# Slots of 2048 bytes and four wide ones, contraction rows padded to 128, and a hand order for the first instructions

## The chip, the cores and the metric

The kernel runs on one core of one Trainium2 chip. The metric is the device time of one execution in microseconds (us). The engines are named as the profile names them: PE (matrix engine) with PEld (its weight loads), DVE (vector), ACT (scalar), POOL, and SP, which here only issues transfers. A matmul multiplies a stationary operand (loaded into PE first) by a moving operand that streams through column by column.

## What is computed

Three blocks over 256 tokens of width 1024, all in float32: two transformer-like layers, then a third with a state-space mixer.

```python
for i in range(2):
    x = x + 0.5 * swiglu(rms_norm(x, g1[i]), w_in1[i], w_out1[i])        # hidden width 2816
    hn = rms_norm(x, gm[i])
    # layer 0: mLSTM, 4 heads of 128 (values 256); layer 1: windowed attention, 16 query and 2 key heads of 64
    y = concat(token_heads(hn @ w_a_or_b), memory_heads(xq, mem_k, mem_v))
    x = x + y @ w_o[i]
    x = x + 0.5 * swiglu(rms_norm(x, g2[i]), w_in2[i], w_out2[i])
h = x + hybrid_mixer(rmsnorm(x))     # state-space scan of 32 heads, short convolutions, gates
h = h + swiglu_2(rmsnorm(h))
return rmsnorm(h)
```

In the windowed attention each of two 128-token blocks scores `s = q k^T` per head, masks it, takes a softmax with a sink, and multiplies by the values. In the state-space scan every head needs `exp(min(acum[l] - acum[s], 0))`, for which one row of cumulative decays per head is spread over all partitions.

## The kernel before, in words

**Weights and products.** Every weight matrix is cut into chunks of up to [128, 1024] float32. `load` (L313) issues a chunk's transfer on SP into one of five `raw` tiles; `prepare` (L321) makes two parts of it, `whi` (ACT copy, rounded to fp32r, L329) and `wlo` (DVE subtraction, L330 through the helper at L122). Activations are split in the same way. A product is three fp32r matmuls: hi·hi, hi·lo, lo·hi. In `gemm` (L396) the activation is stationary and 512 weight columns move (L423 to L425); in `gemm_ch` (L434) the weights are stationary and 256 tokens move (L445 to L447); in `gemm_hidden` (L564) they are stationary and the hi and lo activations move side by side (L574, 512 columns) or the hi ones alone (L575, 256).

**Where operands lie.** SBUF is dealt out in the order of the pools: constants, `wpool` (raw, whi, wlo, 4096 bytes each per partition), `xtp` (two `xt` tiles of 8192 bytes, the transposed normalised activations), `sp` (31 slots under one tag "s"), small tiles. A tag's slots all have the size of its widest tile. `slot()` asks for 512 floats, 2048 bytes, but `v_evac` (L844) asks the same tag for 514 floats, 2056 bytes, so the slots stand more than 2056 bytes apart, while whi, wlo and xt stand at multiples of 2048 bytes from each other. A stationary piece is 128 floats, so pieces within a tile are 512 bytes apart. Products whose activation is a transposed, normalised input take it from `xt`; those after a hidden layer, an attention or a gate take it from slots (`operand_block`, L463).

**Order.** Nothing loops at run time. The Python order is a priority; the Tile scheduler orders the instructions of each engine, adds the waits, and hands a slot to a tile when one is free. Small work (attention, scan) is put between the gemms' matmuls by hand-set paces: `tick` (L365) after every second weight entry, `defer(n, ...)` for n ticks later, `later` and `pipeline` for generators.

**The first instructions** (L751 to L776): `load_x(0)` and two rows of gains on SP, two chunks by `prepare(2)` (which also issues six chunk loads), `load_x(1)` behind them on SP, 8 + 12 warm-up matmuls on PE (L762), the spread of the gains (L766), and per 128 tokens `norm_residual`: squares on ACT (L523), a power on POOL (L513), two scalings on DVE (L131), four transposes and a split per half (L454 to L461). `ffn_in` then takes its first eight chunks as one group: all eight for the first 128 tokens, then all for the others.

**Small contractions.** A matmul's contraction rows are its operands' partitions. Three kinds use fewer than 128: the windowed scores (L1061, 64 rows, plain float32; heads of one parity per unit, since even heads lie in partitions 0 to 63 of the transposed queries and odd ones in 64 to 127), the spread of the mLSTM stabiliser (L857, 4 rows), and the spread of the decays (L1278, 64 rows, fp32r). L1278 runs in 16 units of two matmuls, L1061 in 16 units of two or four, L857 once in each of 4.

Of the kernel before, what the change touches and what calls it, by code (L numbers as in the profile page):

```python
# [27 lines left out]
WBUFS = 9  # L28
N_SLOTS = 31
PACE_A = 0.5  # L30
# [55 lines left out]
def hybrid_kernel(ctx: ExitStack, tc: tile.TileContext, *aps, names=None):  # L86
# [7 lines left out]
    xtp = ctx.enter_context(tc.tile_pool(name="xtp", bufs=2))  # L94
    sp = ctx.enter_context(tc.tile_pool(name="sp", bufs=N_SLOTS))
    tp = ctx.enter_context(tc.tile_pool(name="tp", bufs=1))
    mm = ctx.enter_context(tc.tile_pool(name="mm", bufs=4, space=PSUM))
# [4 lines left out]
    def nm(s):  # L102
        uid[0] += 1
        return f"{s}_{uid[0]}"

    def slot(dtype=F32):
        return sp.tile([P, 512], dtype, tag="s", name=nm("s"))

    def tiny():
# [34 lines left out]
    identr = const.tile([P, P], F32R, name="identr")  # L144
    act.copy(out=identr, in_=ident)
    ones = const.tile([P, P], F32, name="ones")
# [174 lines left out]
    def prepare(upto):  # L321
        while prepared[0] < min(upto, len(plan)):
            c = plan[prepared[0]]
            load(prepared[0] + RAW)
            prepared[0] += 1
            c.hi = wpool.tile([P, 1024], F32R, tag="whi", bufs=WBUFS, name=nm("whi"))
            c.lo = wpool.tile([P, 1024], F32R, tag="wlo", bufs=WBUFS, name=nm("wlo"))
            n = max(off + w for _, _, off, w in c.entries)
            act.copy(out=c.hi[:, 0:n], in_=c.raw[:, 0:n])  # L329
            tt(c.lo[:, 0:n], c.raw[:, 0:n], c.hi[:, 0:n].bitcast(F32), ALU.subtract)  # L330

# [130 lines left out]

    def operand_block(op, tok, k0, src, nk, delay=2):  # L463
        def go():
            hi, lo = slot(F32R), slot(F32R)
            split_t(src, nk, [x[:, 0:nk * P].rearrange("p (a b) -> p a b", a=nk) for x in (hi, lo)])
            for i in range(nk):
                op.parts[tok, k0 + i] = (hi[:, i * P:(i + 1) * P], lo[:, i * P:(i + 1) * P])
        defer(delay, go)
# [111 lines left out]

    def ffn_in(blocks, xop):

# [3 lines left out]
        def evac(t, key, ps):  # L587
            if key == "g":
                keep[t] = slot()
                act.activation(out=keep[t], in_=ps, func=AF.Silu)  # L590
            else:
                tt(keep[t], keep[t], ps, ALU.mult)
                operand_block(h, t, 0, keep[t], 4, D_FFN)
        gemm(blocks[0], xop, evac, [blocks[0][0:FIRST], blocks[0][FIRST:]] if FIRST < 8 else [blocks[0]])

# [158 lines left out]
    for j in range(2):  # L754
        nc.sync.dma_start(out=g_row[j * 32:j * 32 + 1, :], in_=A["ffn1_norm_g"][0:1, j * 512:(j + 1) * 512])
    prepare(2)
    load_x(1)
    warm = bank()

    def warm_up(n):  # L760
        for _ in range(n):
            pe.matmul(out=warm[:, 0:P], lhsT=ones, rhs=ones, start=True, stop=True)  # L762
    warm_up(WARM[0])
    for j in range(2):
        gains.append(bank())
        pe.matmul(out=gains[j], lhsT=ones[j * 32:j * 32 + 1, :], rhs=g_row[j * 32:j * 32 + 1, :], start=True, stop=True)  # L766

    warm_up(WARM[1])

    def fill(t):  # L770
        norm_residual(t, gains, xop)
    for t in range(2):
        fill(t)
    defer(30, lambda: later(load_parameters()))
    pace[0] = 0.25
    h = ffn_in(S["f1in0"], xop)  # L776
    xop, fill = norm_after(A["mix_norm_g"][0])
# [19 lines left out]
    gg, efloor, fcum = little(), little(), little()  # L797
    m_t = slot()

    def gate_chain():  # L800
# [43 lines left out]
    def v_evac(t, key, ps):  # L844
        s = sp.tile([P, 514], F32, tag="s", name=nm("v"))
        act.copy(out=s[:, 1:513], in_=ps)
        pool_e.memset(s[:, 0:1], 1.0)
        pool_e.memset(s[:, 513:514], 1.0)
        v_t[t, int(key[1])] = s

    def score_head(hh):
        while len(k_t) <= hh // 2:
# [3 lines left out]
        bc = bank()  # L856
        pe.matmul(out=bc[:, 0:SEQ], lhsT=ident[0:4, hh:hh + 1].to_broadcast([4, P]), rhs=m_t[0:4, 0:SEQ],  # L857
                  start=True, stop=True)
# [147 lines left out]
    pace[0] = PACE_B  # L1006
    bkt, bv = slot(), slot()
    kv_ready = set()
    qts = {}

    def kv_evac(t, key, ps):
# [8 lines left out]
        def go():  # L1020
            tk = transposes(kd, 2)
            dve.tensor_copy(out=bkt.rearrange("p (g t) -> p g t", g=2)[:, :, t * P:(t + 1) * P],
                            in_=tk[:, 0:SEQ].rearrange("p (g t) -> p g t", g=2))
            kv_ready.add(t)
        defer(D_KV, go)

    def bq_evac(g):
        def evac(t, key, ps):
            qn = qk_norm(ps, t, 8, b_gq)

            def go():
                tq = transposes(qn, 4)
                q = slot()
                act.copy(out=q, in_=tq)
                qts[t, g] = q
            defer(D_ROPE, go)
        return evac

    def swa_units(t, g):
# [4 lines left out]
        mask = mask_w[:, 1, :] if t == 0 else mask_w.rearrange("p a b -> p (a b)")  # L1044
        sets = [[h0 + par + 2 * i for i in range(per)] for h0 in range(0, 8, 2 * per) for par in range(2)]
        sk = sinks[:, 8 * g:8 * g + 8]
        hold = {}

        def unit(n, hs):
            while (t, g) not in qts or len(kv_ready) <= t:  # L1050
                yield
            qt = qts[t, g]
            if not hold:
# [3 lines left out]
            o = slot()  # L1057
            cols = slice(hs[0], hs[-1] + 1, 2)
            for i, hh in enumerate(hs):
                half = slice(64 * (hh % 2), 64 * (hh % 2) + 64)  # L1060
                pe.matmul(out=s[:, i * w:(i + 1) * w], lhsT=qt[half, (hh // 2) * P:(hh // 2 + 1) * P],  # L1061
                          rhs=bkt[half, g * SEQ:g * SEQ + w], start=True, stop=True)
            for i, hh in enumerate(hs):
# [50 lines left out]
    def z_evac(half):  # L1114
        def evac(t, key, ps):
            s = slot()
            act.activation(out=s, in_=ps, func=AF.Silu)
            sz[t, 2 * half + int(key[1])] = s
        return evac
    gemm(S["z0"], xop, z_evac(0), [S["z0"][0:FIRST], S["z0"][FIRST:]] if FIRST < 8 else [S["z0"]])  # L1120

    dt_, acum, toend, eac, dtr = little(), little(), little(), little(), little()
    acs = const.tile([P, 2, 2, 32], F32R, name="acs")
    act_t = const.tile([64, SEQ], F32R, name="act_t")
    pick = const.tile([64, 32], F32R, name="pick")

# [17 lines left out]
    def step_chain():  # L1144
# [29 lines left out]
        for c in range(2):  # L1174
            pe.matmul(out=at_[0:64, c * P:(c + 1) * P], lhsT=acs[:, c, :, :].rearrange("p b c -> p (b c)"), rhs=identr,
                      start=True, stop=True)
        act.copy(out=act_t, in_=at_[0:64, 0:SEQ])
        tt(pick, ident[0:64, 0:32], ident[0:64, 32:64], ALU.add)
        steps_done.append(True)
# [88 lines left out]
    def ssd_unit(g, hp):  # L1268
# [7 lines left out]
        for i in range(2):  # L1276
            hd = 8 * g + 2 * hp + i
            pe.matmul(out=sb[:, i * SEQ:(i + 1) * SEQ], lhsT=pick[:, hd:hd + 1].to_broadcast([64, P]), rhs=act_t,  # L1278
                      start=True, stop=True)
# [168 lines left out]
```

## Time and profile before

| | us |
|---|---|
| median of 3 runs (lowest, highest) | 1605.06 (1604.77, 1608.36) |
| the profiled execution | 1604.94 |
| its span, first to last instruction | 1603.2 |
| PE busy | 1583.9 (99%) |
| DVE busy | 1037.7 (65%) |
| ACT busy | 886.1 (55%) |
| POOL busy | 39.7 (2%) |

Matmuls overlap and their ends are modelled, so PE's busy share says that it always had work, not how fast it went; for that one reads the distance from one matmul's start to the next one's. The granted clock was 0.999 of full speed over the span.

### The profile page before, as it was taken

What the parts mean: (1) busy time and instruction counts of PE and PEld (TensorE: products, weight loads), DVE (VectorE), ACT (ScalarE), POOL (GpSimd) and SP (SyncE); (2) the same over time, 40 slices, a digit from 0 to 9 for tenths busy, and PEclk for the clock granted to TensorE, in tenths of its full rate; (3) what the DMA queues carried; (4) which work ended last, traced back from release to release, by engine and by line L of the source; (5) the groups of instructions that cost most, each with busy time, mean ns of one, the idle gap of its engine ahead of it and who ended that gap; (6) DMA issues with size and microseconds to landing.
All of it is one profiled execution on the core that took longest, in us unless ns stands there. A gap on an engine that the chain in (4) does not pass through costs nothing.

```text
span 1603.2 us, 22953 instructions
## 1 busy us (share of the span) xinstructions
PE 1583.9 (99%) x8664; PEld 1355.3 (85%) x8664; DVE 1037.7 (65%) x1632; ACT 886.1 (55%) x1430; POOL 39.7 (2%) x72
## 2 busy tenths in 40 slices
PE   8999999999999999999999999999999999999998
PEld 7888897788888888887788888889899988888886
DVE  6676475657765567747765676468788864577662
ACT  6665365546655455635565655357855653456542
POOL 1000000100000000001100000000000000000000
PEclk9999999999999999999999999999999999999999
DMA  8656374446556546564323666465455566565560
GB/s 281 196 179 229 117 261 143 151 132 210 174 194 223 179 163 202 193 215 165 119 79 115 200 200 223 143 217 180 146 157 154 151 195 185 157 211 170 197 223 28
DMA packets 126467, 282.89 MB, mean 176 GB/s; under 512 B 11774, under 2 KB 23186, under 8 KB 126356
## 3 DMA queue, kind: packets, MB, share of 16 engines
q1 hardware_dynamic: 126356, 281.43, 54.6%
q8 instruction: 68, 1.11, 0.3%
q14 instruction: 43, 0.35, 0.1%
HBM read 280.34 MB, written 1.05 MB: 176 GB/s over the span
## 4 chain that ended last, share of the span: by engine, by line
PE 93%; DVE 2%; issue 1%; DMA 1%; ACT 1%; POOL 1%; SPq 0%; POOLq 0%; DVEq 0%; ACTq 0%
PE ps L574 20%; PE ps L423 15%; PE ps L425 15%; PE ps L424 15%; PE ps L575 11%; PE ps L445 3%; PE ps L446 3%; PE ps L447 3%; PE ps L458 2%; PE ps L1061 1%; PE ps L1303 1%; PE ps L676 1%; POOL t L517 1%; DVE wlo L122 1%; PE ps L1083 1%
## 5 line engine op out<-in xcount | busy, mean ns | idle before, releaser
L122 DVE TENSOR_TENSOR wlo<-raw,whi 128x1024 fp32r<-128x1024 f32 (+1 forms) x521 | 626.2, 1212 | 228.9 <-ACT whi L329 222.3
L329 ACT CAST whi<-raw 128x1024 fp32r<-128x1024 f32 (+1 forms) x521 | 537.5, 1042 | 321.8 <-PE ps L425 226.6
L574 PE MATMUL ps<-xt,whi 128*128 128x512 f32 x1440 | 500.6, 392 | 0.0
L575 PE MATMUL ps<-xt,wlo 128*128 128x256 f32 x1440 | 403.2, 280 | 0.0
L574 PEld LDWEIGHTS ps<-xt,whi 128*128 128x128 f32 x1440 | 269.4, 187 | 59.1
L423 PE MATMUL ps<-whi,s 128*128 128x512 f32 x696 | 277.4, 400 | 0.3 <-ACT s L1380 0.3
L424 PE MATMUL ps<-wlo,s 128*128 128x512 f32 x696 | 274.4, 394 | 0.0
L425 PE MATMUL ps<-whi,s 128*128 128x512 f32 x696 | 274.1, 394 | 0.0
L575 PEld LDWEIGHTS ps<-xt,wlo 128*128 128x128 f32 x1440 | 272.2, 189 | 0.2
L122 DVE TENSOR_TENSOR s<-ps,s 128x256 f32<-128x256 f32 (+1 forms) x218 | 101.3, 468 | 120.3 <-ACT s L600 100.8
L423 PE MATMUL ps<-whi,xt 128*128 128x512 f32 (+2 forms) x448 | 174.2, 389 | 3.2 <-ACT xt L460 1.8
L425 PE MATMUL ps<-whi,xt 128*128 128x512 f32 (+2 forms) x448 | 170.1, 381 | 1.2 <-DVE xt L122 1.2
L424 PE MATMUL ps<-wlo,xt 128*128 128x512 f32 (+2 forms) x448 | 169.8, 379 | 0.0
L423 PEld LDWEIGHTS ps<-whi,s 128*128 128x128 f32 x696 | 130.8, 188 | 31.4 <-DVE s L122 0.8
L425 PEld LDWEIGHTS ps<-whi,s 128*128 128x128 f32 x696 | 130.7, 188 | 30.7
L424 PEld LDWEIGHTS ps<-wlo,s 128*128 128x128 f32 x696 | 130.9, 188 | 28.7
L445 PE MATMUL ps<-xt,whi 128*128 128x256 f32 x448 | 129.1, 288 | 0.0
L122 DVE TENSOR_TENSOR s<-s,s 128x256 f32<-128x256 f32 (+2 forms) x228 | 107.7, 478 | 32.5 <-ACT s L616 18.0
L446 PE MATMUL ps<-xt,whi 128*128 128x256 f32 x448 | 127.0, 284 | 0.0
L447 PE MATMUL ps<-xt,wlo 128*128 128x256 f32 x448 | 126.8, 284 | 0.0
L600 ACT COPY s<-ps 128x256 f32<-128x256 f32 x180 | 66.2, 368 | 86.7 <-PE ps L575 84.8
L423 PEld LDWEIGHTS ps<-whi,xt 128*128 128x128 f32 x448 | 84.4, 188 | 19.9 <-ACT xt L460 2.2
(218 smaller groups left out, 1369.3 us busy)
## 6 DMA issues: line engine op xcount, KB each, us to landing
raw<-in_ffn_w_in_dram SPq DMA_DIRECT2D x160, 512.0 KB, 4.9
raw<-in_ffn_w_out_dram SPq DMA_DIRECT2D x88, 512.0 KB, 4.5
raw<-in_w_in_dram SPq DMA_DIRECT2D x80, 512.0 KB, 3.9
raw<-in_a_w_in_dram SPq DMA_DIRECT2D x24, 512.0 KB, 4.4
raw<-in_w_down_dram SPq DMA_DIRECT2D x22, 512.0 KB, 4.8
raw<-in_ffn_w_in_dram SPq DMA_DIRECT2D x32, 256.0 KB, 4.5
raw<-in_w_ssd_proj_dram SPq DMA_DIRECT2D x16, 512.0 KB, 3.6
raw<-in_w_gate_dram SPq DMA_DIRECT2D x16, 512.0 KB, 5.0
```

Source lines behind the costliest of these rows:

```text
L122: (eng or dve).tensor_tensor(out=o, in0=a, in1=b, op=op)
L329: act.copy(out=c.hi[:, 0:n], in_=c.raw[:, 0:n])
L423: pe.matmul(out=o, lhsT=xh, rhs=wh, start=first, stop=False)
L424: pe.matmul(out=o, lhsT=xh, rhs=wl, start=False, stop=False)
L425: pe.matmul(out=o, lhsT=xl, rhs=wh, start=False, stop=last)
L445: pe.matmul(out=o, lhsT=wh, rhs=xh, start=kt == 0 and j % 2 == 0, stop=False)
L446: pe.matmul(out=o, lhsT=wh, rhs=xl, start=False, stop=False)
L447: pe.matmul(out=o, lhsT=wl, rhs=xh, start=False, stop=kt == nk - 1 and j % 2 == 1)
L458: pe.transpose(out=ps[:, i * P:(i + 1) * P], in_=src[:, i * P:(i + 1) * P], identity=ident)
L574: pe.matmul(out=ps, lhsT=c.hi[:, sl], rhs=xop.both(kt), start=kt == 0, stop=False)
L575: pe.matmul(out=ps[:, 0:SEQ], lhsT=c.lo[:, sl], rhs=xop.mov(kt)[0], start=False, stop=kt == 7)
L600: act.copy(out=dst, in_=ps[:, SEQ:2 * SEQ])
```

## The change

- `v_evac` takes its 514 floats from a new pool `vp` of four slots of 640 floats (2560 bytes); `sp` has 27 slots of 2048 bytes. The four wide slots also hold the first block of each FFN's hidden activations, the first half of the z gate, and the padded keys of the windowed attention.
- The windowed scores: keys are split into hi and lo and stored with zeros in the other half of the partitions (`kpad`), queries are split too; one matmul of 128 rows scores two heads at once, three fp32r matmuls per pair in place of two float32 ones.
- `m_t`, `acs`, `act_t` and `pick` get 128 rows, the added ones zero, so L857 and L1278 contract over 128 rows.
- At the start the gain rows go out on ACT's queue, `load_x(1)` ahead of chunks 2 to 4 on SP, and PE, ACT and DVE run a stretch in program order: first half of the tokens' norm, then per half a chunk's hi part, the split of the activations, the chunk's lo part, then the norm of the other tokens. The first FFN takes three chunks as a group and then each one alone for both token halves.

```diff
-N_SLOTS = 31
+N_SLOTS = 27
+    vp = ctx.enter_context(tc.tile_pool(name="vp", bufs=4))
+    def wide(dtype=F32):
+        return vp.tile([P, 640], dtype, tag="v", name=nm("v"))
-    act.copy(out=identr, in_=ident)
...
-    def operand_block(op, tok, k0, src, nk, delay=2):
+    def operand_block(op, tok, k0, src, nk, delay=2, home=slot):
-            hi, lo = slot(F32R), slot(F32R)
+            hi, lo = home(F32R), home(F32R)
...
-    def ffn_in(blocks, xop):
+    def ffn_in(blocks, xop, ahead=FIRST):
-                operand_block(h, t, 0, keep[t], 4, D_FFN)
-        gemm(blocks[0], xop, evac, [blocks[0][0:FIRST], blocks[0][FIRST:]] if FIRST < 8 else [blocks[0]])
+                operand_block(h, t, 0, keep[t], 4, D_FFN, home=wide)
+        gemm(blocks[0], xop, evac, [blocks[0][0:ahead]] + [[c] for c in blocks[0][ahead:]])
...
-        nc.sync.dma_start(out=g_row[j * 32:j * 32 + 1, :], in_=A["ffn1_norm_g"][0:1, j * 512:(j + 1) * 512])
-    prepare(2)
+        nc.scalar.dma_start(out=g_row[j * 32:j * 32 + 1, :], in_=A["ffn1_norm_g"][0:1, j * 512:(j + 1) * 512])
+    load(2)
     load_x(1)
+    load(RAW)
...
+    with tc.manual_schedule(engines={mybir.EngineType.PE, mybir.EngineType.Activation, mybir.EngineType.DVE}):
+        warm_up(WARM[0])
...
+        warm_up(WARM[1])
+        halves = {}
+        normed(res_half(0), gains, halves.__setitem__)
+        for j in range(2):
+            low = prepare_hi()
+            split_t(halves[j], 4, [xop.hi[j][:, :, 0, :], xop.lo[j][:, :, 0, :]])
+            xop.filled.add((0, j))
+            low()
+        act.copy(out=identr, in_=ident)
+        norm_residual(1, gains, xop)
-    h = ffn_in(S["f1in0"], xop)
+    h = ffn_in(S["f1in0"], xop, 3)
...
     m_t = slot()
+    pool_e.memset(m_t[:, 0:SEQ], 0.0)
-        s = sp.tile([P, 514], F32, tag="s", name=nm("v"))
+        s = wide()
-        pe.matmul(out=bc[:, 0:SEQ], lhsT=ident[0:4, hh:hh + 1].to_broadcast([4, P]), rhs=m_t[0:4, 0:SEQ],
+        pe.matmul(out=bc[:, 0:SEQ], lhsT=ident[:, hh:hh + 1].to_broadcast([P, P]), rhs=m_t[:, 0:SEQ],
...
-    bkt, bv = slot(), slot()
+    bv = slot()
+    kpad = [[wide(F32R)[:, 0:512].rearrange("p (u t) -> p u t", u=2) for _ in range(2)] for _ in range(2)]
+    for kp in kpad[0] + kpad[1]:
+        pool_e.memset(kp.bitcast(F32), 0.0)
-            dve.tensor_copy(out=bkt.rearrange("p (g t) -> p g t", g=2)[:, :, t * P:(t + 1) * P],
-                            in_=tk[:, 0:SEQ].rearrange("p (g t) -> p g t", g=2))
+            for u in range(2):
+                rows_u = slice(64 * u, 64 * u + 64)
+                for g in range(2):
+                    kh, kl = (kp[rows_u, u, t * P:(t + 1) * P] for kp in kpad[g])
+                    kt = tk[rows_u, g * P:(g + 1) * P]
+                    act.copy(out=kh, in_=kt)
+                    tt(kl, kt, kh.bitcast(F32), ALU.subtract)
-                act.copy(out=q, in_=tq)
-                qts[t, g] = q
+                act.copy(out=qh, in_=tq)
+                tt(ql, tq, qh.bitcast(F32), ALU.subtract)
+                qts[t, g] = (qh, ql)
-        sets = [[h0 + par + 2 * i for i in range(per)] for h0 in range(0, 8, 2 * per) for par in range(2)]
+        sets = [list(range(h0, h0 + per)) for h0 in range(0, 8, per)]
-                pe.matmul(out=s[:, i * w:(i + 1) * w], lhsT=qt[half, (hh // 2) * P:(hh // 2 + 1) * P],
-                          rhs=bkt[half, g * SEQ:g * SEQ + w], start=True, stop=True)
+            kh, kl = (kp[:, :, 0:w] for kp in kpad[g])
+            for i in range(0, per, 2):
+                pair = slice((hs[i] // 2) * P, (hs[i] // 2 + 1) * P)
+                o2 = s[:, i * w:(i + 2) * w].rearrange("p (a b) -> p a b", a=2)
+                pe.matmul(out=o2, lhsT=qh[:, pair], rhs=kh, start=True, stop=False)
+                pe.matmul(out=o2, lhsT=qh[:, pair], rhs=kl, start=False, stop=False)
+                pe.matmul(out=o2, lhsT=ql[:, pair], rhs=kh, start=False, stop=True)
...
-            s = slot()
+            s = slot() if half else wide()[:, 0:512]
...
-    acs = const.tile([P, 2, 2, 32], F32R, name="acs")
-    act_t = const.tile([64, SEQ], F32R, name="act_t")
-    pick = const.tile([64, 32], F32R, name="pick")
+    acs = const.tile([P, 2, 4, 32], F32R, name="acs")
+    pool_e.memset(acs.bitcast(F32), 0.0)
+    act_t = const.tile([P, SEQ], F32R, name="act_t")
+    pick = const.tile([P, 32], F32R, name="pick")
...
-            pe.matmul(out=sb[:, i * SEQ:(i + 1) * SEQ], lhsT=pick[:, hd:hd + 1].to_broadcast([64, P]), rhs=act_t,
+            pe.matmul(out=sb[:, i * SEQ:(i + 1) * SEQ], lhsT=pick[:, hd:hd + 1].to_broadcast([P, P]), rhs=act_t,
```

## Rows read from the trace of the kernel before

**Rows 1.** The page: busy time by engine, and the chain that ended last
```profile
PE 1583.9 (99%) x8664; PEld 1355.3 (85%) x8664; DVE 1037.7 (65%) x1632; ACT 886.1 (55%) x1430; POOL 39.7 (2%) x72
PE 93%; DVE 2%; issue 1%; DMA 1%; ACT 1%; POOL 1%; SPq 0%; POOLq 0%; DVEq 0%; ACTq 0%
```

**Rows 2.** Groups by line and form: shapes, count, busy us, mean ns of one
```profile
L423 PE MATMUL ps<-whi,s 128*128 128x512 f32 x696 | 277.4, 400 | 0.3 <-ACT s L1380 0.3
...
L1061 PE MATMUL ps<-s,s 64*128 64x256 f32 x32 | 10.1, 415 | 0.0
...
L1278 PE MATMUL ps<-act_t,pick 64*128 64x256 f32 x32 | 7.7, 326 | 0.0
...
L1061 PE MATMUL ps<-s,s 64*128 64x128 f32 x32 | 4.6, 285 | 0.7 <-DVE s L1022 0.7
```

**Rows 3.** Timeline of PE, 1300 to 1317 us: first and last of 77 (start, us)
```profile
1299.62 0.39 PE L425 MATMUL ps<-whi,xt 128*128 128x512 f32 x1
...
1316.85 0.39 PE L423 MATMUL ps<-whi,xt 128*128 128x512 f32 x1
```

**Rows 4.** Timeline of PE, 1550 to 1590 us: first and last of 175
```profile
1549.61 0.40 PE L423 MATMUL ps<-whi,s 128*128 128x512 f32 x1
...
1589.92 0.39 PE L423 MATMUL ps<-whi,s 128*128 128x512 f32 x1
```

**Rows 5.** Timeline of PE around one unit of L1278
```profile
1182.78 0.29 PE L446 MATMUL ps<-xt,whi 128*128 128x256 f32 x1
1182.90 0.40 PE L447 MATMUL ps<-xt,wlo 128*128 128x256 f32 x2
1183.23 0.50 PE L1278 MATMUL ps<-act_t,pick 64*128 64x256 f32 x2
1183.66 0.39 PE L445 MATMUL ps<-xt,whi 128*128 128x256 f32 x1
1183.88 0.28 PE L446 MATMUL ps<-xt,whi 128*128 128x256 f32 x1
```

**Rows 6.** Timeline of PE around one unit of L1061
```profile
819.81 0.62 PE L425 MATMUL ps<-whi,s 128*128 128x512 f32 x2
820.36 1.13 PE L1061 MATMUL ps<-s,s 64*128 64x256 f32 x4
821.42 0.50 PE L423 MATMUL ps<-whi,s 128*128 128x512 f32 x1
821.75 0.40 PE L424 MATMUL ps<-wlo,s 128*128 128x512 f32 x1
```

**Rows 7.** The chain that ended last, pieces: start, us, what
```profile
774.03 1.08 PE ps L1061 x8
...
828.36 0.86 PE ps L719 x4
```

**Rows 8.** Timeline of all engines, the first 15 us
```profile
7.51 1.23 DVE L122 TENSOR_TENSOR wlo<-raw,whi 128x1024 fp32r<-128x1024 f32 x1 [2.00 <-ACT whi L329]
...
8.65 0.74 DVE L131 SCALAR_TENSOR_TENSOR s<-xres,t,ps 128x512 f32<-128x512 f32 x1
...
9.34 1.08 SPq L137 DMA_DIRECT2D xres<-in_x_dram  x2
...
13.86 1.28 DVE L122 TENSOR_TENSOR xt<-ps,xt 128x512 fp32r<-128x512 f32 x2
...
14.60 0.73 PE L425 MATMUL ps<-whi,xt 128*128 128x512 f32 x2 [1.18 <-DVE xt L122]
```

**Rows 9.** Timeline of all engines where the windowed attention begins
```profile
771.05 0.42 DVE L1022 COPY s<-ps 128x256 f32<-128x256 f32 x1
...
771.53 1.16 PE L1061 MATMUL ps<-s,s 64*128 64x128 f32 x8 [0.67 <-DVE s L1022]
```

**Rows 10.** Timeline of all engines, inside a unit of the scan
```profile
1184.40 0.63 ACT L1289 ACTIVATE s<-s 128x512 f32<-128x512 f32 x1
...
1185.07 1.29 DVE L122 TENSOR_TENSOR s<-s,s 128x512 f32<-128x512 f32 x2 [1.38 <-ACT s L1289]
```

More of the change, by code (lines that the diff above doesn't have):

```diff
@@ L322, in prepare, with prepare_hi @@
         while prepared[0] < min(upto, len(plan)):
[L323 to L330, printed above, removed]
+            prepare_hi()()
+    def prepare_hi():
+        c = plan[prepared[0]]
+        load(prepared[0] + RAW)
+        prepared[0] += 1
+        c.hi = wpool.tile([P, 1024], F32R, tag="whi", bufs=WBUFS, name=nm("whi"))
+        c.lo = wpool.tile([P, 1024], F32R, tag="wlo", bufs=WBUFS, name=nm("wlo"))
+        n = max(off + w for _, _, off, w in c.entries)
+        act.copy(out=c.hi[:, 0:n], in_=c.raw[:, 0:n])
+        return lambda: tt(c.lo[:, 0:n], c.raw[:, 0:n], c.hi[:, 0:n].bitcast(F32), ALU.subtract)
     index = {}
@@ L762, in warm_up @@
             pe.matmul(out=warm[:, 0:P], lhsT=ones, rhs=ones, start=True, stop=True)
[L763 to L773, printed above, removed]
+    with tc.manual_schedule(engines={mybir.EngineType.PE, mybir.EngineType.Activation, mybir.EngineType.DVE}):
+        warm_up(WARM[0])
+        for j in range(2):
+            gains.append(bank())
+            pe.matmul(out=gains[j], lhsT=ones[j * 32:j * 32 + 1, :], rhs=g_row[j * 32:j * 32 + 1, :],
+                      start=True, stop=True)
+        warm_up(WARM[1])
+        halves = {}
+        normed(res_half(0), gains, halves.__setitem__)
+        for j in range(2):
+            low = prepare_hi()
[4 more added lines that the diff above has]
+        norm_residual(1, gains, xop)
     defer(30, lambda: later(load_parameters()))
     pace[0] = 0.25
-    h = ffn_in(S["f1in0"], xop)
+    h = ffn_in(S["f1in0"], xop, 3)
     xop, fill = norm_after(A["mix_norm_g"][0])
@@ L1032, in go @@
                 tq = transposes(qn, 4)
-                q = slot()
-                act.copy(out=q, in_=tq)
-                qts[t, g] = q
+                qh, ql = slot(F32R), slot(F32R)
+                act.copy(out=qh, in_=tq)
+                tt(ql, tq, qh.bitcast(F32), ALU.subtract)
+                qts[t, g] = (qh, ql)
             defer(D_ROPE, go)
@@ L1051, in unit @@
                 yield
-            qt = qts[t, g]
+            qh, ql = qts[t, g]
             if not hold:
@@ L1057, in unit @@
             o = slot()
-            cols = slice(hs[0], hs[-1] + 1, 2)
-            for i, hh in enumerate(hs):
-                half = slice(64 * (hh % 2), 64 * (hh % 2) + 64)
-                pe.matmul(out=s[:, i * w:(i + 1) * w], lhsT=qt[half, (hh // 2) * P:(hh // 2 + 1) * P],
-                          rhs=bkt[half, g * SEQ:g * SEQ + w], start=True, stop=True)
+            cols = slice(hs[0], hs[-1] + 1)
+            kh, kl = (kp[:, :, 0:w] for kp in kpad[g])
[5 more added lines that the diff above has]
+                pe.matmul(out=o2, lhsT=ql[:, pair], rhs=kh, start=False, stop=True)
             for i, hh in enumerate(hs):
@@ L1174, in step_chain @@
         for c in range(2):
-            pe.matmul(out=at_[0:64, c * P:(c + 1) * P], lhsT=acs[:, c, :, :].rearrange("p b c -> p (b c)"), rhs=identr,
+            pe.matmul(out=at_[:, c * P:(c + 1) * P], lhsT=acs[:, c, :, :].rearrange("p b c -> p (b c)"), rhs=identr,
                       start=True, stop=True)
-        act.copy(out=act_t, in_=at_[0:64, 0:SEQ])
-        tt(pick, ident[0:64, 0:32], ident[0:64, 32:64], ALU.add)
+        act.copy(out=act_t, in_=at_[:, 0:SEQ])
+        tt(pick, ident[:, 0:32], ident[:, 32:64], ALU.add)
         steps_done.append(True)
```

## The prediction

> **What bounds the kernel now.** I read the page's busy times and the chain that ended last first, then PE's groups, then PE's timeline in single stretches. PE is busy 99% of the span and holds 93% of the chain [rows 1]; DVE and ACT have a third and more to spare. So the end moves by what PE's own sequence loses or gains, and work on another engine counts only where PE waits for it. A full busy bar doesn't mean that PE runs at one pace: the reader should look at the distance between starts. Where the stationary operand comes from `xt`, 77 matmuls of 512 columns take (1316.85 - 1299.62)/76 = 226.7 ns each [rows 3]; where it comes from a slot, the same shape with the same moving tiles takes (1589.92 - 1549.61)/174 = 231.7 ns [rows 4]. And a short contraction costs more than its columns: see below. The profiled execution is 1604.94 us, 1.7 over its span and 0.1 below the median of the three runs; the sum is made against it, and a difference of about 0.3% (4.8 us) is what a measurement of this kernel can tell from none.
>
> **Slots of 2048 bytes.** Weights, `xt` and (after) slots then stand at multiples of 2048 bytes from each other, the pieces within them at multiples of 512; the wide slots' 2560 bytes are five times 512. Before, each slot stood a little further off. The number of affected matmuls is 3 x 696 = 2088 (L423, and as many at L424 and L425) [rows 2]. Why an odd offset costs 5.0 ns the profile doesn't say; a load of the next stationary piece runs beside the stream of the moving one, and I take it that the two reads get in each other's way at some offsets. The nearest row for the new placement is `xt` itself, whose pieces also stand at multiples of 512 bytes from the weights: 226.7. Gain 2088 x 5.0 ns = **10.4 us**, all on PE's path. Bounds: nothing (if something else than the offset makes slots slow), and a loss of as much, 10.4 (if equal offsets within 2048 bytes, hi and lo in the same place, are bad in a way that `xt`, whose hi and lo are 1024 bytes apart, avoids). I take the full gain, because `xt` shows all multiples of 512 among its pieces and holds one pace through 77 matmuls.
>
> The Trainium skill speaks against this term: "SBUF — State Buffer", section "SBUF: two separate sides", says that "PE, ACT, and DVE's dedicated pair never wait on anyone", and "TensorE: Matmul & The Clock Gate", "Step-by-step: what each phase is for", that loading the next weights takes no read bandwidth from the running matmul. By that rule an address can't matter and the term is zero, the first rival below. The trace doesn't settle it: the two paces differ, but no row shows an address.
>
> **Short contractions.** Around one unit of L1278, from 1182.90 to 1183.88 five matmuls of 256 columns start (two L447, two L1278, one L445): 0.98 us where the pace before and after is 0.12 each, 0.60 in all [rows 5]. The two matmuls of 64 rows aren't slow in themselves; the one before them, the first, the last and the one behind each lose about 0.1. So a change in the number of rows costs 0.38 us for going in and out. Around a unit of L1061: 819.81 to 821.75 is 1.94 us for three of 512 columns at 0.232 and four L1061; at the pace of the same form with 128 rows, 0.86 for four [rows 7], that would be 1.56: again 0.38 [rows 6]. With 128 rows everywhere, this goes. There are 16 units of L1061, 16 of L1278 and 4 of L857, 36; a few stand directly behind each other and share a change, so I count 34 x 0.38 = **12.9 us** (bounds: 30 runs, 11.4; 36, 13.7). The columns of L857 and L1278 stay as they are, and rows of zeros stream for nothing. The added clearing on POOL hides: POOL is busy 2% [rows 1]. Transposes of 4 and 32 rows stay.
>
> **The scores' own columns.** Before: 32 records of 256 columns at 0.86/4 = 0.215, and 32 of 128 at (1.08 - 0.20)/8 = 0.11 (the 0.20 are the first's and the last's share of the change) [rows 2, 7]: 6.9 + 3.5 = 10.4 us. After: for the first block 24 fp32r matmuls of 256 columns at 0.12 [rows 5], for the second 24 of 512 at 0.23 [rows 3, 4]: 2.9 + 5.5 = 8.4. Gain **2.0 us**.
>
> **What the scores add elsewhere.** Each query block gets a DVE subtraction of 128x512, 0.64 us (1.28 for two) [rows 8]; each key block gets four ACT copies and four DVE subtractions in place of one DVE copy of 0.42, for which PE already waits 0.67 [rows 9]. Behind them in DVE's queue stand the chunk's lo part and the next query's norm, for which PE also waits. Two subtractions of queries come ahead of the first score (1.3), and the key chain is at most 4 x 0.42 = 1.7 long where it was 0.42 (a 64x128 piece isn't dearer than 128x256). Upper bound 1.3 + 1.3 = 2.6, lower bound zero (PE has other matmuls queued there). I take a **loss of 2.0**, nearer the top, since PE stood waiting on this very chain. The second query half comes later, under the other attention units, at no cost.
>
> **Fewer slots.** 27 for 31, and the wide four aren't for all. In the FFNs the hidden block in wide slots makes up for it; in the attention each query block holds two for one. By the code's lifetimes the tightest place is the late scan: 16 slots of split outputs growing, 8 of the short convolution, the last gates and the parts of a group, some 29 at once, when z0's wide slots stand empty. A tile then waits for a slot; PE has the next gemm's matmuls to go on with. I take a **loss of 0.5** (bounds 0 and 3; beyond that is a rival).
>
> **The start.** Now DVE makes a chunk's lo part from 7.51 to 8.74 before the first scaling at 8.65, the second token half is only fetched at 9.34, behind six chunks, and the steady run of matmuls starts at 14.60, when DVE has done the lo activations (13.86) behind two more lo parts [rows 8]. By hand the scalings come first, so the first transposes can start when the warm-up ends, about 1 us earlier, and the lo activations stand ahead of the chunk's lo part, worth about one lo part, 1.23. Against it: chunk 1's hi part now waits for the first split, the three-chunk group needs the other tokens' norm early, with two scalings of 0.74 on DVE ahead of chunk 2's lo part, and at the block's end both token halves are drained at once. The DMAs of the gains leave SP two issues earlier; ACT issues them while it waits for x. I take a **gain of 0.9**, between +3 and -1.5.
>
> **Sum.** 10.4 + 12.9 + 2.0 + 0.9 - 2.0 - 0.5 = 23.7 us less: 1604.94 - 23.7 = 1581.2, say **1581**. What is late next is still PE, at 226.7 ns per matmul of 512 columns.
>
> **Rivals.**
> - *The offset is not the cause.* Slots keep 231.7 ns: 1581 + 10.4 = 1591.5. For it: the two stretches also differ in which weights move and what ACT and DVE read. Against it: shapes, clock and moving tiles are alike. 0.14.
> - *Equal offsets are bad.* Slots get 236.7: 1581 + 20.8 = 1602, within 0.3% of before. Against it: `xt`. 0.05.
> - *The gain is eaten ahead of the scores and at the start.* The key chain's 2.6 comes whole, a similar one behind the second block, and the start loses 1.5 where I count 0.9: 1581 + 8 = 1589. For it: PE's wait of 0.67 [rows 9]. That the hand order doesn't do what it is for lies in this case. 0.10.
> - *Slot hunger in the scan: slower.* If each of the 16 scan units had to wait for a slot until the unit before it has done its exponential and products, 0.63 + 1.29 = 1.92 us [rows 10], and PE stood by, it is 30.7 us: 1581 + 30.7 = 1612. It decides from 1.8 us per unit. For it: 29 against 27 by the code. Against it: only the last units are in the tight place, and PE has gemm work between. 0.05.
> - *All goes better*: start +3 and no loss at the scores: 1581 - 4.6 = 1576. 0.03.
>
> **How the numbers follow.** The forecast has 0.63, its own range about 1577 to 1587. From 1575 to 1592 lie this case, the better one, the third rival and half of the first: about 0.8; the rest is left out. Faster by over 0.3% (under 1600): 0.63 + 0.14 + 0.10 + 0.03 = 0.90; within 0.3%: 0.05; slower: 0.05.
>
> **What would show it.** In the new trace: 512-column matmuls with a stationary slot 226 to 227 ns apart through a down projection; no gap of 0.1 us at the edges of the scores', stabiliser's and decays' matmuls, which have 128 rows; 48 score matmuls in place of 64 records; the first steady run of matmuls near 13 us; PE's wait ahead of the first scores 2 us longer; none in the scan. The prediction is wrong if slots keep 231 ns or more, or if PE shows waits of several us between 1120 and 1320.

## The result, and the profile after

The changed kernel takes 1588.82 us (median of four runs, 1586.37 to 1591.99) against 1605.15 before: a ratio of 0.9893, 95% interval 0.9876 to 0.9910. It is faster by 16.3 us, where 23.7 were forecast: beyond the forecast's own range (1577 to 1587), inside the wider one of 1575 to 1592 that the prediction gives 0.8. The profiled execution is its slowest run, 1591.99 us with a span of 1590.3.

The page of the changed kernel: busy time by engine, and the chain that ended last. They answer [rows 1]:

```profile
PE 1568.8 (99%) x8648; PEld 1352.4 (85%) x8648; DVE 1041.1 (65%) x1642; ACT 888.9 (56%) x1438; POOL 45.4 (3%) x78
...
PE 93%; DVE 3%; ACT 1%; issue 1%; DMA 1%; POOL 1%; POOLq 0%; SPq 0%; DVEq 0%; ACTq 0%
```

PE is still the bound. Its timeline, from the start of the changed kernel to its end, shows what went as predicted, and what did not (start, duration, what; in brackets the wait before):

```profile
6.92 4.59 PE L771 MATMUL ps<-ones 128*128 128x128 f32 x24
11.34 1.04 PE L466 MATMUL ps<-ident,s 128*128 128x128 f32 x8
12.62 0.73 PE L431 MATMUL ps<-whi,xt 128*128 128x512 f32 x2 [0.24 <-ACT xt L468]
...
69.33 0.40 PE L582 MATMUL ps<-xt,whi 128*128 128x512 f32 x1
...
70.39 0.40 PE L582 MATMUL ps<-xt,whi 128*128 128x512 f32 x1
...
224.80 0.44 PE L684 MATMUL ps<-ident,s 128*128 128x128 f32 x2 [2.01 <-DVE s L127]
...
785.34 0.33 PE L684 MATMUL ps<-ident,s 128*128 128x128 f32 x1 [1.20 <-ACT s L1098]
...
1172.08 0.28 PE L453 MATMUL ps<-xt,whi 128*128 128x256 f32 x1
1172.20 0.39 PE L1307 MATMUL ps<-act_t,pick 128*128 128x256 f32 x2
1172.43 0.28 PE L454 MATMUL ps<-xt,whi 128*128 128x256 f32 x1
1172.55 0.28 PE L455 MATMUL ps<-xt,wlo 128*128 128x256 f32 x1
1172.67 1.00 PE L1332 MATMUL ps<-s,s 128*128 128x64 f32 x8
...
1537.70 0.39 PE L431 MATMUL ps<-whi,s 128*128 128x512 f32 x1
...
1577.14 0.39 PE L431 MATMUL ps<-whi,s 128*128 128x512 f32 x1
```

Read from the bottom. The 175 matmuls of [rows 4] now take (1577.14 - 1537.70)/174 = 226.7 ns each, the pace of `xt` in [rows 3], as forecast. Around one unit of the decays, five matmuls of 256 columns start in 1172.67 - 1172.08 = 0.59 us, where [rows 5], around the next unit, had 0.98: the 0.38 is gone there. (The unit of [rows 5] itself now takes 0.71, from 1175.96 to 1176.67; one late start of about 0.1 stays, for a reason that no run shows.) At 785.34 stands a wait of the attention for an exponential that the kernel before did not have; at 224.80 one that it did have, though shorter (1.8). At 69.33 to 70.39 three pairs of the first FFN's hidden gemm take 353 ns each (347 before), and the first line is a warm-up of 24 records that takes 4.59 us.

To see where the 16 us came from, I matched the 7680 matmuls of the gemms one to one (both kernels issue the same number, in the same order but for the first block's chunks and a few in the attention) and took the difference of their starts at the borders of the stages. Us gained (-) or lost (+) against the profile of before, for the profile of the change and of two runs told of below; e7 differs from the change in one tick of the first FFN:

| stage, in the time of before | after | e1, the change again | e7 |
|---|---|---|---|
| start and first block, to 38 | +1.6 | +0.7 | -1.9 |
| rest of the first FFN's hidden gemm, to 145 | +2.2 | +2.2 | +1.9 |
| its down projection, to 191 | -1.1 | -1.1 | -1.1 |
| mLSTM with the stabiliser, to 267 | +0.2 | -2.1 | -1.7 |
| to 732 (no attention, no scan) | -3.3 | -3.4 | -3.3 |
| windowed attention, to 872 | -3.2 | -3.3 | -3.3 |
| to 1121 | -1.2 | -1.3 | -1.2 |
| scan with the decays, to 1306 | -5.3 | -5.3 | -5.3 |
| to the end | -2.7 | -2.8 | -2.7 |
| sum | -12.9 | -16.2 | -18.6 |

All that differs between the three by more than 0.3 lies in the first and the fourth line. Most of it is the clock, below. In the first line, 0.9 of what the first profile loses against e1 is no clock: PE waits 0.69 us for DVE at 28.12 there, behind a weight chunk for which ACT had waited 1.21, and in the other two it doesn't.

### The profile page after: what moved, and what is told of

It reads as the page before. It is cut to its first block, busy times and chain, and to the rows that moved or that the text cites. A ratio compares the mean times of both kernels' runs of the same rounds, so it can differ in the third digit from the quotient of the medians.

```text
span 1590.3 us, 22969 instructions
## 1 busy us (share of the span) xinstructions
PE 1568.8 (99%) x8648; PEld 1352.4 (85%) x8648; DVE 1041.1 (65%) x1642; ACT 888.9 (56%) x1438; POOL 45.4 (3%) x78
## 4 chain that ended last, share of the span: by engine, by line
PE 93%; DVE 3%; ACT 1%; issue 1%; DMA 1%; POOL 1%; POOLq 0%; SPq 0%; DVEq 0%; ACTq 0%
PE ps L582 21%; PE ps L433 15%; PE ps L431 15%; PE ps L432 15%; PE ps L583 11%; PE ps L453 3%; PE ps L454 3%; PE ps L455 3%; PE ps L466 2%; POOL t L525 1%; DVE wlo L127 1%; PE ps L1332 1%; PE ps L684 1%; DVE s L127 1%; PE ps L771 1%
## 5 line engine op out<-in xcount | busy, mean ns | idle before, releaser
L431 PE MATMUL ps<-whi,s 128*128 128x512 f32 x616 | 243.1, 395 | 1.4 <-ACT s L468 1.1
L433 PE MATMUL ps<-whi,s 128*128 128x512 f32 x616 | 240.4, 390 | 0.0
L432 PE MATMUL ps<-wlo,s 128*128 128x512 f32 x616 | 240.1, 390 | 0.0
L127 DVE TENSOR_TENSOR s<-ps,s 128x256 f32<-128x256 f32 (+1 forms) x212 | 97.0, 461 | 114.5 <-ACT s L608 102.3
L431 PEld LDWEIGHTS ps<-whi,s 128*128 128x128 f32 x616 | 115.7, 188 | 25.3 <-ACT s L468 1.3
L433 PEld LDWEIGHTS ps<-whi,s 128*128 128x128 f32 x616 | 115.6, 188 | 24.2
L432 PEld LDWEIGHTS ps<-wlo,s 128*128 128x128 f32 x616 | 115.7, 188 | 23.1
```

Of the source, the lines that this page charges most:

```text
L127: (eng or dve).tensor_tensor(out=o, in0=a, in1=b, op=op)
L431: pe.matmul(out=o, lhsT=xh, rhs=wh, start=first, stop=False)
L432: pe.matmul(out=o, lhsT=xh, rhs=wl, start=False, stop=False)
L433: pe.matmul(out=o, lhsT=xl, rhs=wh, start=False, stop=last)
```

## The experiments

Medians, with the ratio to the kernel before in the same set of runs. The sets are e1, e2, e4 and e6_shift32 (before: 1605.3 us), e3, e5, e7 and e8 (1605.9), and the other four (1605.8).

| run | what | us | ratio, 95% interval |
|---|---|---|---|
| e1_again | the change, unaltered | 1588.66 | 0.9888 (0.9875 to 0.9902) |
| e2_layout | before + placement alone | 1597.09 | 0.9946 (0.9934 to 0.9959) |
| e4_oldstart | change without its start | 1589.19 | 0.9894 (0.9879 to 0.9909) |
| e6_shift32 | change, slots 32 bytes on | 1598.61 | 0.9957 (0.9944 to 0.9970) |
| e3_rows | before + 128-row stabiliser and decays | 1601.63 | 0.9973 (0.9964 to 0.9983) |
| e5_oldscores | change with the old scores | 1589.82 | 0.9903 (0.9888 to 0.9918) |
| e7_onetick | change, two stops in one tick | 1586.00 | 0.9879 (0.9866 to 0.9893) |
| e8_dist3 | change, units three steps apart | 1593.15 | 0.9923 (0.9910 to 0.9935) |
| e9_onestop | e7, one stop moved out | 1587.31 | 0.9886 (0.9873 to 0.9898) |
| e10_nolow | change without the scores' low parts | 1585.95 | 0.9873 (0.9860 to 0.9886) |
| e11_pace | e9, attention spread out | 1595.84 | 0.9940 (0.9927 to 0.9952) |
| e6c_shift256 | change, slots 256 bytes on | 1587.79 | 0.9887 (0.9874 to 0.9900) |

**e1_again**: the change, no edit.

> The changed kernel once more, unaltered, as the level that the variants beside it are held against. Its first profiled execution spent 353.6 ns on each pair of hidden matmuls of the first FFN (512 and 256 columns), where the other four FFNs took 346.7; that is 2.0 us over 288 pairs. If this belongs to that one execution, the pairs of the first FFN take 347 here and the time is 1586 to 1588 us. If it belongs to the change (its start), they take 353 to 354 again and the time stays at 1588 to 1590.

The pairs took 353 to 354 ns again, so the long rhythm belongs to the change; and yet this profiled execution is 3.3 us shorter than the first one, for another reason, told under the clock.

**e2_layout**: of the diff, `N_SLOTS`, the pool `vp`, `wide` and its homes alone.

```diff
-N_SLOTS = 31
+N_SLOTS = 27
-        s = sp.tile([P, 514], F32, tag="s", name=nm("v"))
+        s = wide()
```

> The kernel before with the new placement alone: 27 slots 2048 bytes apart and four wide ones of 2560. Theory, after the two traces: the 2088 matmuls with a stationary slot go from 231.7 to 227 to 228 ns, 3.7 to 4.7 ns each, 8 to 10 us: 1595 to 1597. The prediction had 10.4 - 0.5 = 9.9. Rival (what is quicker in the changed kernel is not owed to the placement): slots stay at 231 to 232 ns and the time at 1604 to 1606.

8.2 us less. In the trace the 2088 slot-stationary matmuls gain 9.4 us together: the 2011 that run steadily (the next gemm matmul starts within 260 ns) go from 231.7 to 227.1 ns on average. The rest was lost in the mLSTM, where this execution met the clock drop that is told below. Its runs at a mean granted clock of 0.999, 1595.46 and 1595.95 us, are 9.4 to 9.9 below the median of before; the two longest, 1598.6 and 1598.7, had 0.996.

**e6_shift32 and e6c_shift256**: the slots' pool is pushed on by a tile of 8 and of 64 floats.

```diff
+    gap = ctx.enter_context(tc.tile_pool(name="gap", bufs=1))
     sp = ctx.enter_context(tc.tile_pool(name="sp", bufs=N_SLOTS))
+    pool_e.memset(gap.tile([P, 8], F32, name="gap"), 0.0)
```

> The changed kernel with all slots moved on by 32 bytes: still 2048 and 2560 bytes apart, but no longer a multiple of 512 bytes away from the weights and from xt. If the offset from the weights decides, stationary slots take 231 to 232 ns again and the time rises by 8 to 10 us. If the distance of the slots from each other decides, they stay at 227 to 228 and the time doesn't move.

> The changed kernel with all slots moved on by 256 bytes: half of the 512 bytes that one stationary piece takes. If only multiples of 512 from the weights are good, stationary slots take 231 to 234 ns as with the shift by 32 and the time is 1597 to 1600; if 256 will do, 227 and 1588 to 1589.

The first and last of the same 175 matmuls, on PE's timeline of e6_shift32:

```profile
1543.04 0.40 PE L433 MATMUL ps<-whi,s 128*128 128x512 f32 x1
...
1583.64 0.40 PE L433 MATMUL ps<-whi,s 128*128 128x512 f32 x1
```

and of e6c_shift256:

```profile
1534.01 0.39 PE L433 MATMUL ps<-whi,s 128*128 128x512 f32 x1
...
1573.45 0.39 PE L433 MATMUL ps<-whi,s 128*128 128x512 f32 x1
```

That is 40.60/174 = 233.3 ns with 32 bytes and 39.44/174 = 226.7 with 256, and in time 10 us lost and none. The slots' distance from each other is the same in both, so where they lie decides, and 256 bytes will do as well as 512. Whether it is their offset from the weights and `xt` or their own address (a multiple of 256 bytes or not) these runs can't tell, since weights and `xt` never moved. The Trainium skill, "SBUF — State Buffer", section "SBUF: two separate sides", has PE waiting for no one in its reads; these two runs differ from the change only in the address of the slots and of the pools behind them, and the measurement decides: an address can cost a matmul of 512 columns 6.6 ns.

**e3_rows**: of the diff, the clearing of `m_t` and the 128-row stabiliser, `acs`, `act_t` and `pick` alone.

```diff
-            pe.matmul(out=sb[...], lhsT=pick[:, hd:hd + 1].to_broadcast([64, P]), rhs=act_t,
+            pe.matmul(out=sb[...], lhsT=pick[:, hd:hd + 1].to_broadcast([P, P]), rhs=act_t,
```

> The kernel before with the 128-row stabiliser and decays alone (20 of the 36 units); slots, scores and start as before. By the prediction's price 16 x 0.38 + 3 x 0.38 = 7.2 us less: 1597.9. By the traces of the changed kernel against that with the layout alone, where the scan gained 4.9 us on its 16 units and the stabiliser's part of the mLSTM between 0 and 2: 1598 to 1600. Rival (the gain there is owed to the slots, or turns into waits): under 3 us, 1602 or more.

4.3 us less, between the two. The trace tells more. From the matmul ahead of each run of decays to the second one behind it, the 15 runs (two units share one) are 0.19 to 0.40 us shorter than before, 5.0 together; the three runs of the stabiliser 0.31 to 0.49, 1.2 together. That is 0.33 and 0.40 per run where 0.38 was forecast. But the third FFN's hidden gemm, on which nothing was changed, ran in the long rhythm here and gave 1.8 back (between 579 and 686 us of before). Four of its 512-column matmuls, on PE's timeline of e3_rows:

```profile
640.12 0.40 PE L574 MATMUL ps<-xt,whi 128*128 128x512 f32 x1
...
640.48 0.40 PE L574 MATMUL ps<-xt,whi 128*128 128x512 f32 x1
...
640.83 0.40 PE L574 MATMUL ps<-xt,whi 128*128 128x512 f32 x1
...
641.18 0.40 PE L574 MATMUL ps<-xt,whi 128*128 128x512 f32 x1
```

Three pairs in 1.06 us, 353 ns each, as in the first FFN of the change.

**e5_oldscores**: the scores' part of the diff taken back (keys in one slot, 64 rows, fp32).

> The changed kernel with the 64-row fp32 scores of the kernel before (32 records of 256 and 32 of 128 columns of line 1061, keys in one slot), all else as changed. By the prediction's terms the new scores are worth 12 to 13 fewer row changes x 0.38 + 2.0 - 2.0, some 4.6 to 6 us: this would be 1593.5 to 1594.5. Theory after the traces: the new scores' gain of 4.8 us at their own matmuls is partly paid back in PE waits for the softmax chain (0.3 to 1.3 us each, 1.5 to 3 in sum), so only 3 to 3.5 are left: 1591.5 to 1592.5.

1.2 us more than e1 and 3.8 more than e7 by the medians. By the traces the new scores bring 3.0 from 732 to 872 us (e5 gains 0.3 there, e1 and e7 3.3), against 6.1 in the prediction (16 x 0.38 + 2.0 - 2.0). PE's waits between 755 and 835 us, in e5_oldscores (waiting line, what it waited for; us in total, times, longest):

```profile
PE ps L684 <- DVE t L133: 1.6, 1, 1.6
PE ps L1076 <- DVE s L1037: 0.6, 1, 0.6
```

and in the changed kernel:

```profile
PE ps L684 <- DVE s L127: 1.8, 2, 1.5
PE ps L684 <- ACT s L1098: 1.4, 2, 1.2
PE ps L431 <- ACT s L468: 1.1, 1, 1.1
PE ps L1088 <- issue: 0.5, 1, 0.5
PE ps L1088 <- DVE s L127: 0.2, 1, 0.2
```

2.2 us there, 5.0 here: the shorter scores come to stand waiting for the softmax. DVE's timeline in the changed kernel shows why the exponential of 785 us was late:

```profile
782.59 0.28 DVE L1092 CUSTOM_DVE_ANT_0 s<-ps,mask_w 128x128 f32<-128x128 f32 x1
...
782.80 0.68 DVE L668 TENSOR_REDUCE t<-s 128x8 f32<-128x512 f32 x1
783.40 0.15 DVE L127 TENSOR_TENSOR t<-t,rows 128x4 f32<-128x4 f32 x1
783.47 1.22 DVE L127 TENSOR_TENSOR wlo<-raw,whi 128x1024 fp32r<-128x1024 f32 x1
784.60 0.16 DVE L131 TENSOR_SCALAR t<-t 128x4 f32<-128x4 f32 x1
```

The unit's maxima are there at 783.5. The negation that the exponential needs (L131) is tiny, but a chunk's lo part of 1.22 us stands ahead of it in DVE's queue. That isn't new, though: in the kernel before, a lo part stands ahead of the same negation, and PE didn't wait there.

```profile
780.83 0.15 DVE L122 TENSOR_TENSOR t<-t,rows 128x4 f32<-128x4 f32 x1
780.90 1.22 DVE L122 TENSOR_TENSOR wlo<-raw,whi 128x1024 fp32r<-128x1024 f32 x1
782.03 0.16 DVE L126 TENSOR_SCALAR t<-t 128x4 f32<-128x4 f32 x1
```

So the queue makes the exponential late in both; what the change altered is how much PE and DVE have to do until then, and the next run tells DVE's part.

**e10_nolow**: leaves out the low parts of queries and keys (the high queries stand in for the low, the low keys are zeros); the matmuls stay.

```diff
-                tt(ql, tq, qh.bitcast(F32), ALU.subtract)
-                qts[t, g] = (qh, ql)
+                qts[t, g] = (qh, qh)
-                    tt(kl, kt, kh.bitcast(F32), ALU.subtract)
```

> The changed kernel without the low parts of the attention's queries and keys: DVE's four subtractions of 128x512 and sixteen of 64x128 are left out, the matmuls stay (the low keys are zeros, the high queries stand in for the low ones). It measures what the scores' added DVE work costs. Theory: PE's waits for the softmax chain in the attention are owed to it; DVE has 4 x 0.69 + 16 x 0.29 = 7.4 us less to do, PE's waits there fall from 5 us to the 2 of the kernel with the old scores, and 2 to 3 us are gained: 1586. Rival (the chain of exp and reduction would be late anyway, since the units' matmuls have become shorter): under 1 us.

The expectation miscounted: eight subtractions of the keys stand in the trace, so DVE has 4 x 0.69 + 8 x 0.29 = 5.1 us less to do, not 7.4. PE's waits fell to 2.6 us, nearly the 2 that were expected:

```profile
PE ps L684 <- DVE t L133: 1.6, 1, 1.6
PE ps L684 <- ACT s L1096: 1.0, 2, 0.8
```

and the attention gains 6.6 us instead of 3.3 between the same matmuls. So the added DVE work costs 3.4 us of PE's time (2.4 of it seen as waits); it is the cause of what is missing in this stage. Of the waits for the exponential, 1.0 of the 1.4 stay even here: that part would be there without the added work, as the rival said.

**e8_dist3 and e11_pace**: two tries to cover these waits.

```diff
-DIST_B = 2
+DIST_B = 3
```

> The changed kernel with the attention's units three steps apart in place of two, so that each unit's softmax has the matmuls of one more unit ahead of its transposes. Theory (PE waits there for the softmax chain on DVE and ACT): the waits of 0.3 to 1.3 us between 780 and 810 us go, and up to 3 us come back: 1585.7 to 1587. Rival (the chain's throughput or PSUM banks set the pace there, not its length): no change or up to 2 us slower.

```diff
-PACE_B = 0.7
+PACE_B = 0.6
```

> The kernel of e9 with the attention's steps spread over more gemm matmuls (0.6 steps per tick in place of 0.7). Theory: more of the next gemm stands between an attention unit's steps, PE waits less for the softmax chain, 1 to 2 us less than e9. Rival: the last units then come after the gemm that covered them, and it is the same or 1 to 3 us slower.

Both are slower than their like in the same set, e8 by 7.1 us against e7 (which differs by one more line; by the ratios it is 5.6 against the change itself) and e11 by 8.5 against e9, more than their rivals said. Their waits only move, and some get longer (2.2 us at 795.58 in e8, 2.3 at 793.89 in e11). The windows of e8_dist3 (stretch, length, then busy us and count of PE, PEld, DVE, ACT, POOL; granted clock; DMA share, GB/s) show what follows them:

```profile
790.00:795.00 5.00, 2.39 (x18) 1.83 (x16) 2.90 (x11) 2.83 (x8) 1.01 (x1) 1.00 0.67 208
795.00:800.00 5.00, 4.02 (x21) 3.65 (x22) 3.64 (x19) 2.80 (x11) 1.01 (x1) 0.65 0.04 16
800.00:805.00 5.00, 5.00 (x30) 4.71 (x30) 1.85 (x15) 3.05 (x14) 0.00 (x0) 0.67 0.01 3
805.00:810.00 5.00, 5.00 (x30) 4.22 (x30) 2.71 (x12) 3.30 (x11) 0.00 (x0) 1.00 0.00 0
```

PE was busy for 2.39 us of five, and then the granted clock was 0.65 and 0.67 on average: with 0.50 for 1.2 GHz, some 7 of these ten us at the lower level, which is 3.4 us lost. e11 has 0.76 and 0.56 from 790 to 800. e1 has no such stretch.

**e4_oldstart**: the start of the diff taken back (gains on SP, no hand order, the first gemm in one group of eight).

> The changed kernel with the start of the kernel before: gains on SP, the order of the first instructions left to the scheduler, the first gemm in groups of eight chunks. Theory: the hand order costs 1.6 to 2.1 us by the end of the first block instead of saving the 0.9 that was predicted, and perhaps the 2.0 us of the first FFN's hidden matmuls too, so this is 1.5 to 4 us faster than the changed kernel. Rival (the prediction): 0.9 us slower than the changed kernel.

0.5 us slower than e1: neither, and within what these runs can tell. Its first FFN has the short rhythm (pairs of 347 ns).

**e7_onetick and e9_onestop**: where the stops for transposes fall in the first FFN's hidden gemm.

```diff
-                operand_block(h, t, 0, keep[t], 4, D_FFN, home=wide)
+                operand_block(h, t, 0, keep[t], 4, D_FFN + (ahead < FIRST and t == 0), home=wide)
```

> The changed kernel with the first FFN's two sets of transposes of its first hidden block in one tick, one directly behind the other (the first token half's set one tick later). In the profiles the hidden gemm runs in one of two rhythms: 230 + 117 ns per pair, or a period of three pairs, 233 + 117 + 241 + 120 + 236 + 113 (353.6 on average); each stop for a set of transposes between pairs has changed one into the other. Theory: one stop in place of two leaves the first FFN in the short rhythm, 347 ns, and gives 1.9 us: 1586.7 against 1588.7. Rival (the long rhythm comes from the start itself, or is chance): 353 to 354 ns again, and no change.

```diff
-    defer(30, lambda: later(load_parameters()))
+    defer(16, lambda: later(load_parameters()))
```

> The changed kernel with both sets of transposes of the first hidden block in one tick, as in the run before (e7), and the parameters' two transposes moved from the middle of the hidden gemm to just ahead of it (deferred by 16 ticks in place of 30). In e7 the hidden gemm of the first FFN went over to the short rhythm at the one stop and back to the long one at the parameters' transposes. Theory: with that stop out of the way it stays at 347 ns per pair to its end, 1.9 us less than the changed kernel: 1585 to 1587. Rival (the rhythm isn't set by stops): 353 to 354 again and no change; if the parameters' loads are late, up to 2 us slower.

The theory fell. e7 went into the short rhythm at its one stop and back into the long one at the next (the parameters' transposes); e9, with that one moved out, ran its first thirteen pairs in the short rhythm and went into the long one at its one stop. In the change itself three stops left the long rhythm as it was. From the first pair to the last, e7 and e9 spent 102.4 and 102.5 us, e1 102.7, and the old start 100.5. The intervals of e7 and e9 overlap that of the change.

**The clock, from rows of these runs.** The warm-up of the changed kernel, 24 records from 6.92 to 11.34 us, is in e7_onetick

```profile
6.07 2.94 PE L771 MATMUL ps<-ones 128*128 128x128 f32 x24
8.85 1.04 PE L466 MATMUL ps<-ident,s 128*128 128x128 f32 x8
10.13 0.73 PE L431 MATMUL ps<-whi,xt 128*128 128x512 f32 x2 [0.24 <-ACT xt L468]
```

with the same instructions: 0.112 us per record against 0.213, the ratio of TensorE's two levels, 2.4 and 1.2 GHz. (The row of the granted clock stays at 1.00 there.) Everything behind comes 2.5 us sooner. In all 14 profiles (one of each run, before and after) PE is busy from 1.20 us on. The full pace comes by 8 us in nine of them, before's among them, and between 10.0 and 17.4 us in five: after, e1, e4, e6c and e9. Old and new start stand on both sides, so it isn't the kernel that decides. This agrees with the Trainium skill, "TensorE: Matmul & The Clock Gate", section "What's actually happening": the moment of the rise isn't tied to the kernel's start and differs between runs of one kernel. The spread that the section gives is half a microsecond either way; here it is far wider, from 4.1 us (e11) to 17.4 (e4). The second place is in the mLSTM, where DVE is late for a transpose in every version. Windows of the changed kernel:

```profile
224.00:225.00 1.00, 0.20 (x3) 0.20 (x3) 0.68 (x3) 0.86 (x1) 0.55 (x2) 1.00 0.87 344
225.00:226.00 1.00, 1.00 (x8) 1.00 (x8) 1.00 (x3) 0.32 (x2) 0.00 (x0) 0.72 1.12 279
226.00:228.00 2.00, 2.00 (x12) 2.00 (x11) 1.50 (x3) 1.97 (x3) 0.00 (x0) 0.50 0.96 279
228.00:230.00 2.00, 2.00 (x15) 2.00 (x15) 1.07 (x7) 1.13 (x2) 0.00 (x0) 0.79 1.06 408
```

After the wait of 2.01 us PE runs at 1.2 GHz for some 3.5 us and loses 1.4. e2 shows the same behind a wait of 2.10 (granted clock 0.50 from 222 to 224); e1, e7 and before, with waits of 1.3 to 1.8 there, don't. The length alone doesn't decide: e10 waited 2.65 us in the same place and e11 2.75 at 783.57, and both had 1.00 behind it.

## Where the prediction was right and where not

**Slots of 2048 bytes: mechanism right, 10.4 forecast, 9.4 to 9.7 measured.** Through the down projection the pace is the forecast 226.7 to a tenth; over all 2088 the mean is a little higher, and some 80 of them stand beside transposes or row changes. The rival that doubted the offset is out by the two shifts, and so is the one that held equal offsets bad. What the prediction couldn't say, why an odd offset costs, is still open: the shifts show that it is the address, not by what path. That two reads get in each other's way was taken, and no run shows it.

**Short contractions: right, a little less per run.** Forecast 34 runs x 0.38. Measured 15 x 0.33 + 3 x 0.40 = 6.2 for scan and stabiliser, where 16 x 0.38 + 3 x 0.38 would be 7.2: one run fewer than units, and less where the unit stands beside other short fp32 matmuls, whose own start still costs. (In two runs beside the gemm, that of [rows 5] among them, a start of about 0.1 stays unexplained.) For the scores, edges and own columns together (8.1 forecast): e10 gains 6.64 in the attention, 0.27 of it by its slots, so 6.4 with its own waits counted in.

**What the scores add elsewhere: the step that failed.** 2.0 forecast, 3.4 measured, beyond the upper bound of 2.6. The prediction named the queue on DVE, but priced it only ahead of the first scores and took the second query half to come "at no cost" under the other units. PE's wait ahead of the first scores stayed as long as it was (0.7); the new waits stand in the middle of the attention. e10 shows that 3.4 us go with the added DVE work; that the rest of the waits is there because shorter scores no longer cover the softmax and the lo part in its queue is read from the traces, and no run took it apart.

**The start: 0.9 forecast, about nothing in the end.** Where both have the early clock, the new order is 1.9 us ahead at 38 us (e7 against before), twice the forecast; the steady matmuls start at 12.32 us in e7, where 13 was forecast. Then the first FFN's hidden gemm gives 1.9 to 2.2 back in the long rhythm. No row read from before showed a second rhythm, though its trace has it in the first thirteen pairs of each hidden gemm, and the term had no place for it. e4 against e1 confirms the net: 0.5, in the noise.

**Fewer slots: 0.5 forecast, none seen.** No such wait shows in the scan; the rival of slot hunger is out.

**The sum.** At the same clock the profile of e7 is 18.6 us shorter than before's, where 23.7 were forecast. By the terms above it is scores 6.4 - 3.4 = 3.0 instead of 6.1, rows 6.2 instead of 7.2, slots 9.5 instead of 10.4, and the start 0 instead of 0.9: 18.7 in all. The medians show 16.3. What the medians lack against the 18.6, 2.3, could be the late clock of the start, worth 2.6 in e1's profile against e7's, which the profiles of after and e1 had and that of before had not. How many of the other runs had it isn't known, so this stays open. It would fit that e1's four runs, all at a mean clock of 0.999, stand at 1585.2 and at 1588.7 to 1589.0, and that the profiled one is of the upper three.

The third rival had put a gain eaten ahead of the scores and at the start at 1589. The number fits the result better than the forecast's, but that is luck: nothing is lost ahead of the first scores, and its 8 us count the 2.0 twice that the forecast had already taken off. By its own terms, 0.6 + 2.6 + 2.4, it is 5.6 and 1587.

## What to carry to other kernels

Put stationary operands at multiples of 256 bytes from the moving ones, as the quick runs here had them, and measure the distance between starts, not the busy time: 5 ns on each of 2088 matmuls was the largest term here, and the page showed 99% busy before and after. When matmuls on a chain are made cheaper, price the chain through the engines behind them at its tightest point, and look at what stands in their queues ahead of the small instruction that releases PE. Two microseconds of waiting can cost nearly as much again (1.4 behind 2.0 in the mLSTM), since the clock may fall behind them; and one profile isn't enough for a start, which differs by 2.6 us between two profiles here through the clock alone.

## What the runs showed that I had not expected

- **Two rhythms of one instruction stream.** Pairs of 512 and 256 columns run at 347 ns (230 + 117) or with a period of three pairs, 233 + 117 + 241 + 120 + 236 + 113, 353 each. Nearly all hidden gemms start in the long one and leave it at the stop behind their thirteenth pair. With the new start the first FFN spends most of its pairs in it in every profile, with the old one in none, and e3's third FFN stayed in it too. By the code the instructions of the pairs are the same; no trace shows addresses. What selects the rhythm is open.
- **An offset of 32 bytes costs 6.6 ns per 512 columns** (233.3 against 226.7), one of 256 bytes nothing.
- **The clock at 1.2 GHz well into the kernel**: 1.4 us lost behind a wait of 2.0 in the mLSTM; and some 7 us long in e8's attention, with PE's waits of 2.2 us and less around it.
